# A GpSimd product for the gate weights of every second token group in a dense expert stage

## The chip, the cores and the metric

The kernel runs on one core of a Trainium2 chip. The metric is the device time of one execution in microseconds. The time before is the median of three runs; the profile is of a further execution of the same program.

## What is computed

The reference is one decoder layer on 512 tokens of width 1024: a sparse-attention head group and a gated linear recurrence side by side, one output projection, a layer norm, then a product-key expert layer (PEER) and a second layer norm. Only the expert layer matters here. Each token picks 128 of 16,384 single-neuron experts (8 heads times 16 picks), with a softmax weight for each pick:

```python
g = jax.nn.softmax(best, axis=-1)
h = jax.nn.gelu(jnp.einsum('td,thkd->thk', xb, u[experts]))
return jnp.einsum('thk,thkd->td', g * h, v[experts])
```

The inputs are float32, and all products below are float32.

## The kernel before, in words

The 512 tokens are four blocks of 128. Two ways of doing the expert layer run beside each other.

Blocks 0 and 1 are gathered (`peer_gather`, L657). For each pick k, GpSimd issues an indirect DMA (`gather`, L639) that fetches one row of 1024 numbers of table u for each of the 128 tokens, and VectorE takes its dot product with the block's activations (L663). Later the rows of table v are gathered and added up with their weights on VectorE (L676). `peer_gather` is a generator; `pump(n)` (L705) takes n rows from it at places written by hand in the rest of the program. The last 52 picks of block 0 go another way (`pe_gather`, L684): ScalarE multiplies the identity by the pick's weights into a diagonal matrix `dg` (L692), and TensorE multiplies the gathered row by it and accumulates (L694, two products of 128x512 for each row). There is one buffer for `dg`.

Blocks 2 and 3 are dense (`dense`, L714). No row is gathered: all 16,384 experts are run over these 256 tokens, and a matrix G of 128 x 128 weights for each token, zero where an expert was not picked, stands for the choice. Two stages follow one another in `dense`:

- The **G stage** (L740 to L764) builds G, four tokens at a time, in 64 groups. The picks lie on the partitions. For each group VectorE makes two one-hot tiles of 128x512 (L747), `og[0]` and `og[1]`, by comparing an iota with the two indices of every pick; both operands lie in SBUF. The picks' gate weights are multiplied into `og[1]`. In even groups ScalarE does that for three of the four tokens (L751, one 128x128 instruction for a token) and VectorE for the fourth (L753); in odd groups ScalarE does all four. TensorE then multiplies `og[0]` by `og[1]` token by token into a PSUM bank `gb` (L756), and ScalarE copies the bank of the group before into G (L734). Every third group pumps one gathered row of block 1 (GPUMP, L737; 22 in all), and 30 of the rows of `pe_gather` for block 0 are spread over the first 60 groups (L761).
- The **dense stage** (L819 to L838) streams u and v from memory in 128 rounds, splits them into two halves for precision on ScalarE and VectorE (L772, L774), and runs their products (L783, L803). It pumps the remaining gathered rows evenly.

`og[0]` has four buffers, which the u tiles of the dense stage share; `og[1]` has six. The gathered rows of both kinds share four buffers here. The two PSUM banks of the groups alternate.

The order of instructions on each engine comes from a planner that simulates the program with costs of its own and places each instruction when its operands and buffers are free; lines marked to keep program order (the dot products, the sums over gathered rows, some loads) stay in order among themselves. Each engine then runs its list strictly in order, GpSimd's gathers included, and waits by semaphores.

GpSimd does little elementwise work in the kernel before: four products of 128x512 (L267, the recurrence's gate by a norm weight that is broadcast) and four copies of 128x512 (L468), all long ahead of the G stage. L418, L419 and L676 are further VectorE work that stands near these in the trace.

Of the kernel before, what the change touches and what calls it, by code (L numbers as in the profile page):

```python
# [9 lines left out]
F32 = mybir.dt.float32  # L10
# [5 lines left out]
ALU = mybir.AluOpType  # L16
# [9 lines left out]

HGB = 5
GB = 4
UB = 4
VB = 3  # L30
HLB = 6
# [8 lines left out]
PEK2 = 38  # L40
PEPRE = 8
PEG = 60

GACTS = (3, 4)

GPUMP = 3

# [4 lines left out]
def tile_decoder_layer(ctx, tc, a, out):  # L52
    nc = tc.nc

    cst = ctx.enter_context(tc.tile_pool(name="cst", bufs=1))
    gat = ctx.enter_context(tc.tile_pool(name="gat", bufs=5))
# [66 lines left out]
    def layer_norm(ys, os_, g, b, nm):  # L123

        n = len(ys)
        mv = cst.tile([128, n, 2], F32, name="mv" + nm, tag="ln_mv", bufs=2)
        parts = [y if isinstance(y, list) else [y[:, k * 512:(k + 1) * 512] for k in range(2)] for y in ys]
        for i in range(n):
            st = cst.tile([128, 2, 6], F32, name=f"st{nm}_{i}", tag="ln_st", bufs=2)
            for k in range(2):  # L130
                nc.vector.bn_stats(st[:, k, :], parts[i][k])  # L131
            nc.vector.bn_aggr(mv[:, i, :], st)
        ve = cst.tile([128, n], F32, name="ve" + nm, tag="ln_ve", bufs=2)
        nc.vector.tensor_scalar(ve, mv[:, :, 1], EPS, None, op0=ALU.add)
        r = rsqrt(ve, n, nm)
        for i, o in enumerate(os_):
            if isinstance(ys[i], list):
                for k in range(2):
                    sl = slice(k * 512, k * 512 + 512)
                    nc.vector.scalar_tensor_tensor(o[:, sl], parts[i][k], mv[:, i, 0:1], g[:, sl],  # L140
                                                   op0=ALU.subtract, op1=ALU.mult)
            else:
                nc.vector.scalar_tensor_tensor(o, ys[i], mv[:, i, 0:1], g, op0=ALU.subtract, op1=ALU.mult)
            nc.vector.scalar_tensor_tensor(o, o, r[:, i:i + 1], b, op0=ALU.mult, op1=ALU.add)  # L144
# [487 lines left out]
    def gather(table, b, k, nm):  # L632
        n = nth[0] % (GB + len(lent))
        nth[0] += 1
        if n < GB:
            t = gat.tile([128, 1024], F32, name=f"g{nm}{b}_{k}", tag="g", bufs=GB)
        else:
            t = cst.tile([128, 1024], F32, name=f"g{nm}{b}_{k}", tag=lent[n - GB])
        nc.gpsimd.indirect_dma_start(out=t, out_offset=None, in_=table,  # L639
                                     in_offset=bass.IndirectOffsetOnAxis(ap=idx[b][k // 64][:, k % 64:k % 64 + 1], axis=0))  # L640
        return t

    def ln2_consts(nm):
        gb = []
        for i in range(2):
            t = gat.tile([128, 1024], F32, name=f"ln2_{nm}_{i}", tag="g", bufs=GB)
            nc.sync.dma_start(t, a["ln2"][None, i, :].to_broadcast([128, 1024]))
# [36 lines left out]
    def pe_gather(n, p):  # L684

        while 0 not in weighted:
            pump(1)
        ks = [pe_left.pop(0) for _ in range(n)]
        for k in ks:
            g = gather(a["v"], 0, k, "v")  # L690
            dg = gat.tile([128, 128], F32, name=f"dg{k}", tag="dg", bufs=1)
            nc.scalar.mul(dg, ident, gate[:, 0, k:k + 1])  # L692
            for i in range(2):
                nc.tensor.matmul(p[i], dg, g[:, i * 512:(i + 1) * 512], start=(k == ks[0]), stop=(k == ks[-1]))  # L694
            if k != ks[-1]:
                yield
        for i in range(2):
            y = hs[0][:, i * 512:(i + 1) * 512]
            nc.vector.tensor_tensor(y, y, p[i], op=ALU.add)
        yield  # L700
# [4 lines left out]
    def pump(n):  # L705
        while n > 0 and todo:
            try:
                if not next(todo[0]):
                    return
                n -= 1  # L710
            except StopIteration:
                todo.pop(0)

    def dense(den, dps):  # L714
# [5 lines left out]
        for i, b in enumerate(DENSE):  # L720
# [4 lines left out]
            nc.scalar.copy(t[:, 0:3, :].rearrange("p a b -> p (a b)"), p[:, :384])  # L725
            tr[b] = [t[:, n, :] for n in range(3)]
        pw = pe_gather(PEK2, [dps.tile([128, 512], F32, name=f"pw{n}", tag=f"acc0_{n}") for n in range(2)])
        for _ in range(PEPRE):
            next(pw)
# [3 lines left out]
        def evacuate(t0, p):  # L733
            nc.scalar.copy(G[:, :, t0:t0 + 4].rearrange("p j t -> p t j"), p)  # L734

        def pump_some(t0):
            if t0 // 4 % GPUMP == 0:  # L737
                pump(1)

        for t0 in range(0, T, 4):  # L740
            p = dps.tile([128, 4, 128], F32, name=f"gb{t0}", tag="gb", bufs=2)
            x = tr[DENSE[t0 // 128]]
            c = t0 % 128
            og = [den.tile([128, 4, 128], F32, name=f"og{t0}_{n}", tag=tag, bufs=bufs)
                  for n, (tag, bufs) in enumerate((("u", UB), ("hl", HLB)))]
            for n in range(2):
                nc.vector.tensor_tensor(og[n], iota[:, None, :].to_broadcast([128, 4, 128]),  # L747
                                        x[n][:, c:c + 4, None].to_broadcast([128, 4, 128]), op=ALU.is_equal)
            gact = GACTS[t0 // 4 % len(GACTS)]
            for tt in range(gact):  # L750
                nc.scalar.mul(og[1][:, tt, :], og[1][:, tt, :], x[2][:, c + tt:c + tt + 1])  # L751
            if gact < 4:
                nc.vector.tensor_tensor(og[1][:, gact:, :], og[1][:, gact:, :],  # L753
                                        x[2][:, c + gact:c + 4, None].to_broadcast([128, 4 - gact, 128]), op=ALU.mult)
            for tt in range(4):
                nc.tensor.matmul(p[:, tt, :], og[0][:, tt, :], og[1][:, tt, :], start=True, stop=True)  # L756
            if t0:
                evacuate(t0 - 4, last)
            last = p
            pump_some(t0)  # L760
            while pdone < PEK2 and pdone < PEPRE + (t0 // 4 + 1) * (PEK2 - PEPRE) // PEG:  # L761
                next(pw)
                pdone += 1
# [13 lines left out]
        def into_hidden(j, n, hp):  # L777
            u = den.tile([128, 512], F32, name=f"u{j}_{n}", tag="u", bufs=UB)
            nc.sync.dma_start(u.rearrange("p (k i) -> p k i", k=4), a["ut"][j, :, n * 4:n * 4 + 4, :])
            uh, ul = split(f"u{j}_{n}", u)  # L780
            for q, (ut, ht) in enumerate(((uh, hTl), (uh, hTh), (ul, hTh))):
                for k in range(4):
                    nc.tensor.matmul(hp, ut[:, k * 128:(k + 1) * 128], ht[n][:, k, :],  # L783
                                     start=(n + q + k == 0), stop=(n == 1 and q == 2 and k == 3))
# [18 lines left out]
                    nc.tensor.matmul(acc[i][n], wt[:, sl], vt, start=(j == 0 and q == 0), stop=(j == 127 and q == 2))  # L803

        def residual():
            ia = gat.tile([128, 128], F32, name="ia", tag="dg", bufs=1)
            nc.scalar.mul(ia, ident, ALPHA)
            for i in range(nb):
                for n in range(2):
                    for c in range(4):  # L810
                        for t in (hTl, hTh):
                            nc.tensor.matmul(acc[i][n][:, c * 128:(c + 1) * 128],
                                             t[n].bitcast(F32)[:, c, i * 128:(i + 1) * 128], ia,
                                             start=False, stop=False)
# [4 lines left out]
        for j in range(129):  # L819
# [18 lines left out]
            ws = ws_new  # L838
        ys = [gat.tile([128, 1024], F32, name=f"y{b}", tag="g", bufs=GB) for b in DENSE]
        layer_norm(acc, ys, gb[0], gb[1], "l2_dense")  # L840
# [3 lines left out]
    def stage(blocks, xT):  # L844
# [31 lines left out]
        if blocks != [0]:  # L876
            lent.clear()
            for part, tags in (("h", ("hx0", "hx1")), ("l", ("hs2", "hs3"))):
                hT_parts[part] = [cst.tile([128, 4, 256], F32R, name=f"hT{part}{i}", tag=tag) for i, tag in enumerate(tags)]
            for k in range(0, 8, 2):  # L880
                x = hT[:, k:k + 2, 128:384]
                th, tl = [hT_parts[part][k // 4][:, k % 4:k % 4 + 2, :] for part in "hl"]
                nc.scalar.copy(th, x)
                nc.vector.tensor_tensor(tl, x, th.bitcast(F32), op=ALU.subtract)
            for _ in pe_gather(PEK1, [bank(f"pv{i}", "hg") for i in range(2)]):
                pass
# [6 lines left out]
    with tc.tile_pool(name="den", bufs=1) as den, tc.tile_pool(name="dps", bufs=1, space=PSUM) as dps:  # L893
        dense(den, dps)
# [48 lines left out]
```

## Time and profile before

| what | value |
|---|---|
| median of 3 runs | 1611.0 us (1610.07 to 1612.66) |
| the profiled execution | 1606.46 us |
| its span, first to last instruction | 1604.6 us |
| busy: TensorE, VectorE, ScalarE, GpSimd | 1446.5, 1383.7, 708.0, 673.9 us |
| the G stage, first one-hot tile to the end of its last | 702.55 to 831.4 us |
| the dense stage | about 838 to 1590 us |

In the profile PE is TensorE, PEld its weight loads, DVE is VectorE, ACT is ScalarE and POOL is GpSimd. Shares over the whole span hide the stages: ScalarE is busy for 44% of the span, but in the two slices of 40 that lie wholly in the G stage it is busy for 9 tenths or more, and less in the dense stage. So a change in one stage is read from windows of that stage, and from the rows of single instructions in it. Instructions of ScalarE, VectorE and TensorE overlap by a little, so that the length of one is more than the distance from its start to the next one's. The number in square brackets behind a row is the idle time of the engine ahead of it, with what ended it.

### The profile page before, as it was taken

The numbers are of one execution on the slowest core, as the hardware profiler recorded it, in microseconds if no ns is written. First come the engines' busy times: TensorE is split into PE (matmuls) and PEld (weight loads), VectorE is DVE, ScalarE is ACT, GpSimd is POOL, SyncE is SP. The second block draws the span as 40 slices with busy tenths as digits, with TensorE's granted clock in tenths as the row PEclk, the third lists the DMA queues.
The fourth block names the chain that finished last, engine by engine and source line by source line (L and its number), as shares of the span: only waits on it lengthen the run. The fifth ranks groups of instructions, "written<-read, shape, count | busy, mean of one in ns | idle before, by whom it ended". The sixth has DMA issues, their size and how long they took to land. (4 is left out here: it accounts for less than half of the span.)

```text
span 1604.6 us, 24491 instructions
## 1 busy us (share of the span) xinstructions
PE 1446.5 (90%) x7858; PEld 1087.4 (68%) x7858; DVE 1383.7 (86%) x3263; ACT 708.0 (44%) x1501; POOL 673.9 (42%) x531
## 2 busy tenths in 40 slices
PE   8889899854788899789989999999999999999996
PEld 4568444543444565246668888888898889889995
DVE  4139999799966899998877989999998899999998
ACT  3302331122432122169984555555555555555553
POOL 0004633777744420355433444444443345534440
PEclk9999999855799899899999999999999999999998
DMA  8378987899967770467668999999999999999995
GB/s 291 125 277 301 348 268 232 290 344 330 351 242 255 263 285 11 145 203 222 218 235 301 350 340 337 353 349 352 352 357 326 336 349 362 351 352 350 355 367 189
DMA packets 166161, 467.89 MB, mean 292 GB/s; under 512 B 18576, under 2 KB 18704, under 8 KB 165904
## 3 DMA queue, kind: packets, MB, share of 16 engines
q0 software_dynamic: 73728, 268.47, 48.0%
q1 hardware_dynamic: 92304, 197.86, 34.3%
q8 instruction: 62, 1.02, 0.2%
q14 instruction: 67, 0.55, 0.1%
HBM read 464.16 MB, written 2.10 MB: 291 GB/s over the span
## 5 line engine op out<-in xcount | busy, mean ns | idle before, releaser
L639 POOL DMA_INDIRECT gv<-in_v_dram,idx x256 | 333.1, 1301 | 417.4 <-DVE hs L676 263.3
L639 POOL DMA_INDIRECT gu<-in_u_dram,idx x256 | 330.9, 1293 | 409.8 <-DVE gu L663 259.1
L663 DVE SCALAR_TENSOR_TENSOR gu<-gu,hs 128x1024 f32<-128x1024 f32 x256 | 307.2, 1222 | 28.0 <-DMA gu<-in_u_dram,idx 27.8
L676 DVE SCALAR_TENSOR_TENSOR hs<-gv,gate,hs 128x1024 f32<-128x1024 f32 x204 | 261.4, 1281 | 9.7 <-DMA gv<-in_v_dram,idx 7.8
L772 ACT CAST v_0h<-v 128x512 fp32r<-128x512 f32 x128 | 79.7, 623 | 95.7 <-PE acc L803 60.9
L523 PE MATMUL pq<-hT,wpq 128*128 128x128 f32 (+1 forms) x512 | 121.3, 396 | 0.0
L774 DVE TENSOR_TENSOR u_0l<-u,u_0h 128x512 fp32r<-128x512 f32 x128 | 88.5, 691 | 35.6 <-ACT u_0h L772 32.6
L772 ACT CAST v_1h<-v 128x512 fp32r<-128x512 f32 x128 | 79.5, 621 | 87.7 <-DMA v<-in_v_dram 42.8
L772 ACT CAST u_0h<-u 128x512 fp32r<-128x512 f32 x128 | 79.4, 620 | 78.0 <-PE hp L783 41.1
L803 PE MATMUL acc<-v_0h,wl 128*128 128x512 f32 x256 | 102.0, 399 | 4.9 <-DVE wl L793 4.9
L523 PEld LDWEIGHTS pq<-hT,wpq 128*128 128x128 f32 x512 | 81.2, 201 | 33.4 <-issue 3.9
L803 PE MATMUL acc<-v_0h,wh 128*128 128x512 f32 x256 | 101.0, 395 | 0.0
L772 ACT CAST u_1h<-u 128x512 fp32r<-128x512 f32 x128 | 79.4, 621 | 48.2 <-PE acc L803 44.6
L774 DVE TENSOR_TENSOR v_1l<-v,v_1h 128x512 fp32r<-128x512 f32 x128 | 87.8, 686 | 14.3 <-ACT v_1h L772 13.5
L803 PE MATMUL acc<-v_1h,wh 128*128 128x512 f32 x256 | 99.7, 389 | 0.0
L803 PE MATMUL acc<-v_1h,wl 128*128 128x512 f32 x256 | 99.7, 389 | 0.0
L803 PE MATMUL acc<-v_0l,wh 128*128 128x512 f32 x256 | 99.5, 390 | 0.0
L774 DVE TENSOR_TENSOR u_1l<-u,u_1h 128x512 fp32r<-128x512 f32 x128 | 87.7, 685 | 4.5 <-ACT wh L791 3.5
L783 PE MATMUL hp<-hTl,u_0h 128*128 128x256 f32 x512 | 84.3, 287 | 8.0 <-ACT u_0h L772 8.0
L783 PEld LDWEIGHTS hp<-hTl,u_0h 128*128 128x128 f32 x512 | 76.7, 189 | 20.8 <-ACT u_0h L772 12.4
L774 DVE TENSOR_TENSOR v_0l<-v,v_0h 128x512 fp32r<-128x512 f32 x128 | 88.1, 688 | 2.5 <-ACT v_0h L772 1.6
L783 PE MATMUL hp<-hTh,u_1l 128*128 128x256 f32 x512 | 83.9, 286 | 5.1 <-DVE u_1l L774 5.1
(277 smaller groups left out, 3137.9 us busy)
## 6 DMA issues: line engine op xcount, KB each, us to landing
v<-in_v_dram SPq DMA_DIRECT2D x256, 256.0 KB, 6.2
u<-in_ut_dram SPq DMA_DIRECT2D x256, 256.0 KB, 6.0
wpq<-in_w_pq_dram SPq DMA_DIRECT2D x32, 512.0 KB, 4.7
wo<-in_w_o_dram SPq DMA_DIRECT2D x16, 512.0 KB, 7.6
hfw<-in_w_hf_dram SPq DMA_DIRECT2D x8, 512.0 KB, 6.8
hqw<-in_w_hq_dram SPq DMA_DIRECT2D x8, 512.0 KB, 9.1
hiw<-in_w_hi_dram SPq DMA_DIRECT2D x8, 512.0 KB, 4.9
qaw<-in_w_qa_dram SPq DMA_DIRECT2D x8, 512.0 KB, 5.1
```

What stands on the lines that cost most here:

```text
L523: nc.tensor.matmul(qp[:, :nt], w[:, k, :], hT[:, k, :nt], start=(k == 0), stop=(k == 7))
L639: nc.gpsimd.indirect_dma_start(out=t, out_offset=None, in_=table, in_offset=bass.IndirectOffsetOnAxis(ap=idx[b][k // 64][:, k % 64:k % 64 ...
L663: nc.vector.scalar_tensor_tensor(g, g, 1.0, hs[b], op0=ALU.mult, op1=ALU.mult, accum_out=hd[:, k:k + 1]))
L676: nc.vector.scalar_tensor_tensor(hs[b], g, gate[:, b, k:k + 1], hs[b], op0=ALU.mult, op1=ALU.add))
L772: nc.scalar.copy(h, x)
L774: nc.vector.tensor_tensor(l, x, h.bitcast(F32), op=ALU.subtract)
L783: nc.tensor.matmul(hp, ut[:, k * 128:(k + 1) * 128], ht[n][:, k, :], start=(n + q + k == 0), stop=(n == 1 and q == 2 and k == 3))
L803: nc.tensor.matmul(acc[i][n], wt[:, sl], vt, start=(j == 0 and q == 0), stop=(j == 127 and q == 2))
```

## The change

In the G stage the weights are now applied in one of two ways. In odd groups one GpSimd product of 128x512 multiplies all of `og[1]` by the weights, broadcast along each token's 128 columns. In even groups ScalarE does all four tokens. VectorE's L753 is gone. The buffer of the diagonals `dg` becomes two; the dense stage's `ia`, which uses the same buffer, has two as well.

```diff
+DGB = 2
...
-GACTS = (3, 4)
...
-            dg = gat.tile([128, 128], F32, name=f"dg{k}", tag="dg", bufs=1)
+            dg = gat.tile([128, 128], F32, name=f"dg{k}", tag="dg", bufs=DGB)
...
-            gact = GACTS[t0 // 4 % len(GACTS)]
-            for tt in range(gact):
-                nc.scalar.mul(og[1][:, tt, :], og[1][:, tt, :], x[2][:, c + tt:c + tt + 1])
-            if gact < 4:
-                nc.vector.tensor_tensor(og[1][:, gact:, :], og[1][:, gact:, :],
-                                        x[2][:, c + gact:c + 4, None].to_broadcast([128, 4 - gact, 128]), op=ALU.mult)
+            if t0 // 4 % 2:
+                nc.gpsimd.tensor_tensor(og[1], og[1], x[2][:, c:c + 4, None].to_broadcast([128, 4, 128]), op=ALU.mult)
+            else:
+                for tt in range(4):
+                    nc.scalar.mul(og[1][:, tt, :], og[1][:, tt, :], x[2][:, c + tt:c + tt + 1])
...
-            ia = gat.tile([128, 128], F32, name="ia", tag="dg", bufs=1)
+            ia = gat.tile([128, 128], F32, name="ia", tag="dg", bufs=DGB)
```

## Rows read from the trace of the kernel before

**Rows 1.** Windows, G stage: busy us (instructions), granted clock, DMA share, GB/s

```profile
core 0: us, PE busy (x) PEld busy (x) DVE busy (x) ACT busy (x) POOL busy (x), PEclk, DMA share, GB/s
703.00:833.00 130.00, 121.57 (x632) 82.09 (x632) 112.74 (x207) 128.40 (x319) 60.06 (x54) 1.00 0.71 225
```

**Rows 2.** Groups, 704 to 838 us: count, busy us, mean ns, idle before, releaser

```profile
L747 DVE TENSOR_TENSOR og<-iota,dtr 128x512 f32<-128x512 f32 x126 | 79.8, 687 | 0.8 <-PE gb L756 0.7
L751 ACT ACTIVATE og<-og,dtr 128x128 f32<-128x128 f32 x224 | 74.4, 427 | 0.3 <-DVE og L747 0.2
...
L694 PE MATMUL pw<-gv,dg 128*128 128x512 f32 x128 | 63.0, 614 | 7.2 <-ACT dg L692 7.2
...
L663 DVE SCALAR_TENSOR_TENSOR gu<-gu,hs 128x1024 f32<-128x1024 f32 x22 | 26.9, 1224 | 16.2 <-DMA gu<-in_u_dram,idx 16.2
...
L692 ACT ACTIVATE dg<-ident,gate 128x128 f32<-128x128 f32 x31 | 13.3, 429 | 0.0
```

**Rows 3.** Timeline of ACT: start, length, line, count; idle before in brackets

```profile
792.49 0.39 ACT L692 ACTIVATE dg<-ident,gate 128x128 f32<-128x128 f32 x1
792.79 1.03 ACT L734 COPY G<-gb 128x512 f32<-128x512 f32 x1
793.62 0.96 ACT L751 ACTIVATE og<-og,dtr 128x128 f32<-128x128 f32 x3
794.49 1.04 ACT L734 COPY G<-gb 128x512 f32<-128x512 f32 x1
```

**Rows 4.** Timeline of PE, same stretch

```profile
796.93 1.98 PE L694 MATMUL pw<-gv,dg 128*128 128x512 f32 x4 [0.19 <-ACT dg L692]
798.75 2.06 PE L756 MATMUL gb<-og,og 128*128 128x128 f32 x16
```

**Rows 5.** Timeline of DVE: the stage's first products, one round, the stage's end

```profile
702.55 6.18 DVE L747 TENSOR_TENSOR og<-iota,dtr 128x512 f32<-128x512 f32 x10 [0.60 <-ACT dtr L725]
...
796.76 1.22 DVE L663 SCALAR_TENSOR_TENSOR gu<-gu,hs 128x1024 f32<-128x1024 f32 x1 [0.83 <-DMA gu<-in_u_dram,idx]
...
797.91 0.28 DVE L753 TENSOR_TENSOR og<-og,dtr 128x128 f32<-128x128 f32 x1
798.11 2.52 DVE L747 TENSOR_TENSOR og<-iota,dtr 128x512 f32<-128x512 f32 x4
...
803.13 1.23 DVE L663 SCALAR_TENSOR_TENSOR gu<-gu,hs 128x1024 f32<-128x1024 f32 x1 [0.96 <-DMA gu<-in_u_dram,idx]
...
831.44 0.68 DVE L699 TENSOR_TENSOR hs<-hs,pw 128x512 f32<-128x512 f32 x1
```

**Rows 6.** Windows, dense stage: busy times, clock, DMA share, GB/s, as in group 1

```profile
1400.00:1500.00 100.00, 99.57 (x641) 90.63 (x640) 95.48 (x140) 54.05 (x106) 45.43 (x33) 1.00 0.98 353
```

**Rows 7.** Timeline after the stage: ACT's first cast of the dense stage

```profile
837.13 0.62 ACT L772 CAST u_0h<-u 128x512 fp32r<-128x512 f32 x1 [3.57 <-DMA u<-in_ut_dram]
```

**Rows 8.** Timeline of POOL, HGRN2 gate products of blocks 1 and 2

```profile
274.60 2.50 POOL L267 TENSOR_TENSOR gs<-gs,ghg 128x512 f32<-128x512 f32 x2
```

**Rows 9.** Timeline of POOL, same round as DVE's in group 5

```profile
798.26 1.35 POOL L639 DMA_INDIRECT gu<-in_u_dram,idx  x1 [2.11 <-DVE og L753]
799.91 0.94 POOL L639 DMA_INDIRECT gv<-in_v_dram,idx  x1 [0.31 <-PE gb L756]
804.63 1.15 POOL L639 DMA_INDIRECT gu<-in_u_dram,idx  x1 [3.78 <-DVE gu L663]
```

**Rows 10.** Timeline of DVE over the second of these products

```profile
272.14 1.22 DVE L663 SCALAR_TENSOR_TENSOR gu<-gu,hs 128x1024 f32<-128x1024 f32 x1
...
276.19 2.00 DVE L663 SCALAR_TENSOR_TENSOR gu<-gu,hs 128x1024 f32<-128x1024 f32 x1
```

**Rows 11.** POOL copy, DVE L676 over it; L676's ns min/median/max over all

```profile
430.88 0.97 POOL L468 COPY rex<-rsm 128x512 f32<-128x512 f32 x1
...
431.42 2.83 DVE L676 SCALAR_TENSOR_TENSOR hs<-gv,gate,hs 128x1024 f32<-128x1024 f32 x2
...
L676 DVE SCALAR_TENSOR_TENSOR hs<-gv,gate,hs x204: 1270/1280/1510, 411.2 to 1576.0; 128x1024 f32<-128x1024 f32 x102
```

## The prediction

> **What bounds the kernel now.** I read the windows first, to see which engine fills the G stage. From 703 to 833 us ScalarE is busy for 128.4 of 130 us, TensorE for 121.6, VectorE for 112.7 and GpSimd for 60.1, at full clock [rows 1]. The groups then tell who waits: ScalarE's weights (L751) and diagonals (L692) have next to no idle time ahead of them, while TensorE waits 7.2 us for diagonals and VectorE 16.2 us for gathered rows [rows 2]. So ScalarE sets the pace, and TensorE stands close behind.
>
> Busy times overlap on these engines, so I take the pitch from start to start. ScalarE: three weights from 793.62 to 794.49, 0.29 us each; one evacuation from 792.79 to 793.62, 0.83; one diagonal 0.30 [rows 3]. The stage has 224 weights, 64 evacuations and 30 diagonals: 65.0 + 53.1 + 9.0 = 127.1 us, which is the stage. TensorE: one gathered row's two products take 1.82 us, and two groups' products 2.06 [rows 4]: 30 x 1.82 + 32 x 2.06 = 120.5 us. VectorE: a one-hot tile takes 0.61 us (ten in 6.18, four in 2.52), a dot product with a gathered row 1.15, an L753 multiply 0.20 [rows 5]: 128 x 0.61 + 22 x 1.15 + 32 x 0.20 = 78.1 + 25.3 + 6.4 = 109.8. VectorE's part of the stage runs from 702.55 to 831.44 [rows 5], 128.9 us, so 19 us of it are idle, 16.2 of them waits for gathers.
>
> Behind the stage, TensorE is busy for 99.6 of 100 us in the dense stage [rows 6], and its first operand is loaded into buffers that the G stage gives back, which ScalarE awaits for 3.57 us [rows 7]. Nothing there absorbs a shift; I pass a change of the G stage on to the end one to one.
>
> **What goes.** ScalarE loses 96 of its 224 weights: 27.8 us, leaving 99.3. VectorE loses the 32 multiplies of L753: 6.4 us, leaving 103.4. The second diagonal buffer costs or brings next to nothing: ScalarE did not wait for TensorE to give the first one back (idle before L692: 0.0 [rows 2]); TensorE's 7.2 us came from ScalarE's own queue, and that shortens with the 27.8 us. Were VectorE's and GpSimd's work untouched, TensorE's 120.5 us would be the next bound.
>
> **What is added.** GpSimd gets 32 products of 128x512. The same operation, shape and broadcast is in the kernel: the four at L267 take 1.27 us each, two of them in a row 2.50 [rows 8]. GpSimd has room: 54 gathers at 1.41 us (60.1 us of busy time over 54, and the 0.3 that stands even ahead of one that hardly waits, at 799.91 [rows 9]) and 32 x 1.27 are 76 + 41 = 117 us.
>
> The price lies on VectorE. While the second of these two ran (until 274.60 + 2.50 = 277.10), a dot product that started at 276.19 took 2.00 us, where the one before took 1.22 [rows 8, 10]: 0.78 of the 0.91 us that were left of the GpSimd product were lost to it. The reverse shows inside the G stage, where VectorE's one-hot tiles start at 798.11 and every 0.61 us after [rows 5]. The gather at 799.91, just ahead of the tile boundary at 799.94, took 0.94 us; the one at 798.26 took 1.35 [rows 9], and 798.26 + (1.35 - 0.94) is 798.67, where the tile from 798.11 makes way for that of 798.72. GpSimd waits for the end of a VectorE tile, and VectorE for the end of a GpSimd product. All VectorE work left in the stage is of this kind: one-hot tiles and dot products, both with two operands in SBUF. So GpSimd's products add to VectorE's time; they don't run beside it.
>
> How much of a product VectorE loses has two ends. The copy at L468 (430.88, 0.97 us) ended at 431.85, and the sum that started at 431.42 took 1.51 where 1.28 is usual [rows 11]: 0.23 lost of 0.43, about half, or 0.68 us of a 1.27 us product. The other end is the whole 1.27. The L267 row (0.78 of 0.91) is the same operation, so I take 0.86 x 1.27 = 1.10. The Trainium skill (SBUF — State Buffer, section "SBUF: two separate sides") says that the loser of the port pair is blocked for the other's whole instruction; by that the price is 1.27 and the sum 5.4 us higher. The L267 row has it a little shorter.
>
> **The sum.** VectorE: 103.4 + 32 x 1.10 = 138.6 us against the 128.9 of now: +9.7, with no idle left (ends: 103.4 + 21.8 = 125.2, -3.7; 103.4 + 40.6 = 144.0, +15.1). To this come waits for gathers, now 16.2 us. The ends are none and all of it. The dot product at 803.13 waited 0.96 us, and its gather was issued 4.87 us before at 798.26, once the dot product from 796.76 had given its buffer back [rows 5, 9]. Three groups bring 1.5 products, some 1.6 us more VectorE time between two dot products, less 0.3 for the lost L753, which by itself covers that 0.96. But a product now also stands ahead of gathers in GpSimd's in-order queue, and its 1.27 us, plus up to 0.61 until a tile ends, come on top of the 4.87 for perhaps every second gather. I take some 6 us of waiting, between the ends and nearer none. Together +16 us.
>
> The profiled execution took 1606.5 us (span 1604.6 and 1.9 around it), 4.5 below the median of the runs shown. On it the sum is 1606.5 + 16 = 1622.5; the same shift on the median gives **1627**. The forecast's own range: +6 (a price of 1.0 and no waits) to +31 (the full 1.27 and all 16.2 of the waits): 1617 to 1642.
>
> **Rivals.**
> (a) Faster. The place is the meeting of L747 and the new product; the point that decides is what one product costs VectorE. With no idle left, VectorE keeps today's 128.9 us at (128.9 - 103.4) / 32 = 0.80 us; well below that TensorE decides at 120.5, 8.4 us less than now: 1603. For it: the copy's 0.68, and VectorE's 19 idle us, in which products could fall for free. Against it: the L267 row, and the gather that waited for the tile. The Trainium skill (Advanced Engine Details and Errata, section "VectorE Performance Modes") names only GpSimd and two-port VectorE instructions as blocking each other; by that rule tiles at one element per cycle would be free, and this rival would follow. The dot product of 2.00 us in this trace speaks against it: at 1.15 us for 1024 elements it is not in a doubled mode either, and was blocked. 14%.
> (b) Nothing measurable. Dot products follow one another once in three groups, here after 6.37 us (796.76 to 803.13 [rows 5]), and this loop of gather, landing and release runs at ScalarE's pace already. If products fit into its waits at a price near 0.80, stage and time stay: 1611. 9%.
> (c) Much slower by the queue. GpSimd works in order: a gather that waits for a buffer (3.78 us at 804.63 [rows 9]) holds up the product behind it, and with it TensorE's group and the evacuation. If each of the 22 rounds loses 1 us more this way, it is 22 us on top of +9.7: 1643, with 1637 to 1665 possible. Against it: four one-hot buffers let VectorE work ahead, and the planner puts products and gathers in one order that it foresees. 17%.
> That the change doesn't do what it says has little room: the 96 weights leave ScalarE's queue whatever the planner does, and I give it no chance of its own.
>
> **The numbers.** The forecast (+6 to +31) has 60%. Slower: 60 + 17 = 77%. Faster 14%, same 9%, where 0.2% (3.2 us) is about what a measurement of this kernel can tell from no change. The range 1606 to 1648 holds the forecast, (b) and over half of (c), and leaves out (a) and the upper part of (c), a little under 2 in 10.
>
> **What would show it.** Right: dot products and one-hot tiles in the G stage that take about 1.1 us longer than the 1.22 and 0.69 of now [rows 2], some 32 of them; ScalarE with idle time and some 100 us of work; a stage that ends 10 to 20 us later, with the dense stage unchanged in length. TensorE waits for og from GpSimd. Wrong: L747 tiles at 0.69 us throughout while products run, or the products falling into VectorE's idle time; then TensorE would stand at 120 us with no gaps. Long idle times before the products, with gathers ahead of them, would show (c).

## The result and the profile after

The changed kernel took 1628.05 us (median of 7 executions, 1626.07 to 1634.13), the kernel before 1612.66 us beside it (7 executions, 1609.92 to 1621.38). The ratio is 1.0094, with a 95% interval of 1.0066 to 1.0121: slower by 15.4 us. The median of the kernel before moves from job to job (1612.7, 1621.4, 1636.7, 1618.3 and 1616.7 us in five), so below only ratios within one job are compared, and of the profiles the lengths of stages. Line numbers after are one or two smaller: L747 is now L746, L663 is L662, L692 and L694 are L691 and L693; the weights stand at L749 (GpSimd) and L752 (ScalarE).

Windows of the changed kernel, the stage and 100 us of the dense stage. The columns are those of [rows 1].

```profile
core 0: us, PE busy (x) PEld busy (x) DVE busy (x) ACT busy (x) POOL busy (x), PEclk, DMA share, GB/s
719.00:857.00 138.00, 111.54 (x605) 80.39 (x606) 137.34 (x177) 106.36 (x218) 97.71 (x80) 0.97 0.63 193
1424.00:1524.00 100.00, 98.27 (x629) 89.05 (x628) 95.05 (x138) 53.34 (x104) 47.14 (x34) 1.00 0.97 351
```

Against [rows 1] the engine without idle time is another one: VectorE, busy for 137.3 of 138 us. ScalarE has 32 us of idle time and TensorE 26. The dense stage [rows 6] is as it was.

Groups of the changed kernel from 704 to 862 us, as in [rows 2]: count, busy us, mean ns, idle time before them.

```profile
L746 DVE TENSOR_TENSOR og<-iota,dtr 128x512 f32<-128x512 f32 x128 | 109.7, 918 | 16.1 <-ACT dtr L724 15.4 <-PE gb L754 0.6
...
L693 PE MATMUL pw<-gv,dg 128*128 128x512 f32 x120 | 62.0, 641 | 32.2 <-DMA gv<-in_v_dram,idx 32.2
...
L752 ACT ACTIVATE og<-og,dtr 128x128 f32<-128x128 f32 x128 | 40.8, 390 | 16.5 <-DVE og L746 16.3
L749 POOL TENSOR_TENSOR og<-og,dtr 128x512 f32<-128x512 f32 x32 | 37.4, 1169 | 6.9 <-DVE og L746 2.6 <-PE gb L754 2.5 <-PE pw L693 1.3
...
L662 DVE SCALAR_TENSOR_TENSOR gu<-gu,hs 128x1024 f32<-128x1024 f32 x23 | 30.1, 1311 | 0.0
L691 ACT ACTIVATE dg<-ident,gate 128x128 f32<-128x128 f32 x28 | 10.9, 391 | 26.1 <-PE pw L693 25.9
```

The one-hot tiles went from 687 ns to 918, the dot products from 1224 to 1311. That is 128 x 0.231 + 23 x 0.087 = 31.6 us more VectorE time, 0.99 us for each of the 32 products. The dot products wait for nothing any more (16.2 us before). ScalarE's weights wait for VectorE. Two waits are new and, as the run e2 below shows without any product, come from the second buffer: TensorE's gathered rows wait 32.2 us for their gathers (11.4 of it ahead of the first tile), and VectorE waits 15.4 us for `dtr`, the copy of the transposed picks, ahead of its first tile.

The time of the stages follows from the starts of single instructions: the last one of VectorE's routing (the choice of each token's picks) ahead of the stage, the first and the last one-hot tile, the first and the last product of the dense stage. The two profiles at the right are one more execution of each kernel, taken together (its expectation stands with the experiments).

| us | before | after | difference | before, again | after, again | difference |
|---|---|---|---|---|---|---|
| last routing instruction | 701.7 | 703.1 | +1.4 | 705.9 | 708.6 | +2.7 |
| from there to the first one-hot tile | 0.8 | 15.7 | +14.9 | 8.8 | 16.0 | +7.2 |
| VectorE's part of the stage | 128.9 | 138.4 | +9.5 | 131.8 | 139.8 | +8.0 |
| from its end to the first dense product | 6.4 | 1.2 | -5.2 | 3.9 | 0.4 | -3.5 |
| dense products | 754.1 | 755.8 | +1.7 | 758.6 | 754.0 | -4.6 |
| span | 1604.6 | 1626.9 | +22.3 | 1621.7 | 1631.8 | +10.1 |

The two differences lie on both sides of the medians' +15.4. What they share is +8 to +9.5 in the stage, +7 to +15 ahead of it and -3.5 to -5.2 behind it.

**What a product does.** Timelines of the changed kernel: GpSimd's products first, then VectorE beside them.

```profile
781.56 1.05 POOL L749 TENSOR_TENSOR og<-og,dtr 128x512 f32<-128x512 f32 x1
787.55 1.05 POOL L749 TENSOR_TENSOR og<-og,dtr 128x512 f32<-128x512 f32 x1
...
779.45 3.72 DVE L746 TENSOR_TENSOR og<-iota,dtr 128x512 f32<-128x512 f32 x4
783.09 1.21 DVE L662 SCALAR_TENSOR_TENSOR gu<-gu,hs 128x1024 f32<-128x1024 f32 x1
...
784.23 4.93 DVE L746 TENSOR_TENSOR og<-iota,dtr 128x512 f32<-128x512 f32 x6
```

Four tiles took 2.52 us before [rows 5] and take 3.72 with one product beside them; six take 4.93 where the pitch of 0.61 makes 3.7. Either way some 1.2 us go to a product of 1.05. The dot product with no product beside it keeps its 1.21. Where the product itself took longer (1.16 us and more), the tile beside it took 1.51 instead of 1.91 and lost 0.8; the mean of 0.99 lies between the two.

One product of the 32 met other VectorE work, and it cost nothing (GpSimd, then VectorE):

```profile
844.96 1.04 POOL L749 TENSOR_TENSOR og<-og,dtr 128x512 f32<-128x512 f32 x1 [2.50 <-PE gb L754]
...
844.74 1.27 DVE L698 TENSOR_TENSOR hs<-hs,pw 128x512 f32<-128x512 f32 x2
845.94 0.68 DVE L130 BATCH_NORM_STATS2 stl<-hs 128x6 f32<-128x512 f32 x1
```

The sum L698 reads one of its operands from PSUM, and L130 has one operand. Two sums in 1.27 us is their usual pace (0.68 each, overlapping; the same sum of the kernel before took 0.68 [rows 5]). So it is VectorE's instructions with two operands in SBUF that lose time to a product here. No run was made to vary the operands; the rows of the second profile of the changed kernel and of e8 show the same.

**What stands ahead of the stage.** Timelines of the changed kernel from 692 us on: GpSimd, TensorE, ScalarE, VectorE.

```profile
692.11 11.52 POOL L638 DMA_INDIRECT gv<-in_v_dram,idx  x1 [0.30 <-PE pw L693]
...
707.52 3.75 PE L693 MATMUL pw<-gv,dg 128*128 128x512 f32 x4 [11.38 <-DMA gv<-in_v_dram,idx]
...
715.85 1.95 PE L693 MATMUL pw<-gv,dg 128*128 128x512 f32 x4 [1.85 <-DMA gv<-in_v_dram,idx]
717.64 0.38 PE L722 MATMUL dtp<-ident,ij 128*128 128x128 f32 x2
...
711.37 0.40 ACT L691 ACTIVATE dg<-ident,gate 128x128 f32<-128x128 f32 x1 [12.96 <-PE pw L693]
...
717.91 0.40 ACT L691 ACTIVATE dg<-ident,gate 128x128 f32<-128x128 f32 x1 [3.41 <-PE pw L693]
718.21 0.84 ACT L724 COPY dtr<-dtp 128x384 f32<-128x384 f32 x2
...
703.10 0.23 DVE L619 SCALAR_TENSOR_TENSOR idx<-dc_v,dc_v 128x64 uint32<-128x64 f32 x1
718.76 1.29 DVE L746 TENSOR_TENSOR og<-iota,dtr 128x512 f32<-128x512 f32 x2 [15.43 <-ACT dtr L724]
```

One gather took 11.52 us. TensorE's row (707.52) waited 11.38 us for it, and two more rows stood between that row and the last transposes of the picks (717.64). ScalarE's diagonals (L691) waited for the rows to give a buffer back, and the copy of the transposes, which every one-hot tile needs, stood behind them. In TensorE's order 11 rows stand ahead of the last transposes; in the kernel before it is 5. Nobody moved them by hand: the planner placed them earlier once there were two diagonal buffers.

In the kernel before the same stretch reads as follows (GpSimd, TensorE).

```profile
698.01 4.24 POOL L639 DMA_INDIRECT gv<-in_v_dram,idx  x1 [1.02 <-PE pw L694]
...
698.29 1.99 PE L694 MATMUL pw<-gv,dg 128*128 128x512 f32 x4 [0.55 <-ACT dg L692]
...
701.21 0.33 PE L723 MATMUL dtp<-ident,ij 128*128 128x128 f32 x1 [0.83 <-DVE ij L617]
```

The long gather (4.24 us) belongs to a row behind the transposes, so nothing that the first tile needs waits for it.

**Behind the stage** ScalarE's first cast of the dense stage, which waited 3.57 us for its u tile [rows 7], waits no more (timeline of ScalarE, changed kernel).

```profile
855.74 0.63 ACT L770 CAST u_0h<-u 128x512 fp32r<-128x512 f32 x1
```

### The profile page after: what moved, and what is told of

Same layout as the page of the kernel before. It is cut to its first block, busy times and chain, and to the rows that moved or that the text cites. A ratio compares the mean times of both kernels' runs of the same rounds, so it can differ in the third digit from the quotient of the medians.

```text
span 1626.9 us, 24442 instructions
## 1 busy us (share of the span) xinstructions
PE 1446.2 (89%) x7858; PEld 1095.7 (67%) x7858; DVE 1407.4 (87%) x3231; ACT 687.9 (42%) x1405; POOL 724.2 (45%) x563
## 3 DMA queue, kind: packets, MB, share of 16 engines
q8 instruction: 62, 1.02, 0.3%
## 5 line engine op out<-in xcount | busy, mean ns | idle before, releaser
L638 POOL DMA_INDIRECT gv<-in_v_dram,idx x256 | 348.3, 1361 | 417.5 <-DVE hs L675 264.4
L662 DVE SCALAR_TENSOR_TENSOR gu<-gu,hs 128x1024 f32<-128x1024 f32 x256 | 308.9, 1229 | 11.4 <-DMA gu<-in_u_dram,idx 11.4
L746 DVE TENSOR_TENSOR og<-iota,dtr 128x512 f32<-128x512 f32 x128 | 109.7, 918 | 16.1 <-ACT dtr L724 15.4
L693 PE MATMUL pw<-gv,dg 128*128 128x512 f32 x152 | 77.8, 642 | 41.6 <-DMA gv<-in_v_dram,idx 32.7
```

The costliest lines, as they stand in the source:

```text
L662: nc.vector.scalar_tensor_tensor(g, g, 1.0, hs[b], op0=ALU.mult, op1=ALU.mult, accum_out=hd[:, k:k + 1]))
```

## The experiments

Theory P (port): each GpSimd product stops VectorE for about its own length. Theory D (diagonals): the second buffer of diagonals itself costs time, by the order that it gives. "D1" below is the changed kernel with `DGB = 1`.

**One diagonal buffer with the products** (e1):

```diff
-DGB = 2
+DGB = 1
```

> The changed kernel with one buffer of diagonals, as before the change. Theory P (each GpSimd product takes some 1.1 us from VectorE): the G stage's VectorE part stays at about 138 us. Theory D (the second diagonal buffer is what makes the first one-hot tile start at 718.8 instead of 702.6 us): it starts near 703 again, and the time falls by 6 to 16 us from that of the changed kernel, to 1612 to 1622. Rival (the late start comes from a plan that moved because of the GpSimd products): first tile near 718 and the time of the changed kernel, 1628.

Ratio 1.0074 (1.0040 to 1.0108). Groups, 704 to 862 us:

```profile
L746 DVE TENSOR_TENSOR og<-iota,dtr 128x512 f32<-128x512 f32 x128 | 105.7, 889 | 0.6 <-ACT dtr L724 0.6
...
L662 DVE SCALAR_TENSOR_TENSOR gu<-gu,hs 128x1024 f32<-128x1024 f32 x23 | 32.1, 1394 | 11.2 <-DMA gu<-in_u_dram,idx 11.2
```

The wait ahead of the stage is gone (0.6), and the price stays: 128 x 0.202 + 23 x 0.170 = 29.8 us, 0.93 each. But 11.2 us of waits for gathers are back and the stage takes 140.1 us (with its last tile counted at the usual 0.68), with another 10.6 from its end to the first dense product. So the start near 703 came back as theory D said, but the fall of 6 to 16 us did not come: these waits took the place of the buffer's gap, and by the time alone the two kernels cannot be told apart.

**Two diagonal buffers in the kernel before** (e2):

```diff
-            dg = gat.tile([128, 128], F32, name=f"dg{k}", tag="dg", bufs=1)
+            dg = gat.tile([128, 128], F32, name=f"dg{k}", tag="dg", bufs=2)
...
-            ia = gat.tile([128, 128], F32, name="ia", tag="dg", bufs=1)
+            ia = gat.tile([128, 128], F32, name="ia", tag="dg", bufs=2)
```

> The kernel before with two buffers of diagonals and nothing else. The prediction's step (the second buffer costs or brings next to nothing): within 3 us of the kernel before, first one-hot tile near 703. Theory D: the first tile starts 10 to 16 us later and the time rises by 5 to 15 us. P says nothing of it: tiles stay at 0.69 us.

Ratio 1.0075 (1.0041 to 1.0109), without one product on GpSimd. Groups, 704 to 862 us:

```profile
L747 DVE TENSOR_TENSOR og<-iota,dtr 128x512 f32<-128x512 f32 x128 | 81.3, 685 | 33.0 <-PE gb L756 21.1 <-ACT dtr L725 11.9
...
L694 PE MATMUL pw<-gv,dg 128*128 128x512 f32 x120 | 62.6, 647 | 27.4 <-DMA gv<-in_v_dram,idx 27.3
L639 POOL DMA_INDIRECT gv<-in_v_dram,idx x28 | 31.6, 1128 | 39.5 <-PE pw L694 30.7 <-PE dtp L723 5.4 <-issue 3.0
L663 DVE SCALAR_TENSOR_TENSOR gu<-gu,hs 128x1024 f32<-128x1024 f32 x23 | 28.0, 1217 | 0.0
```

The tiles keep their 0.69 us, the first one waits 11.9 us for `dtr` (again 11 rows stand ahead of the last transposes), and within the stage rows wait for gathers while gathers wait for rows to give their buffers back. The dot products wait for nothing (0.0), with no product in the kernel. The stage takes 135.2 us. Theory D holds, for the gap and inside the stage.

**The product on VectorE**, with two buffers (e3) and with one (e5, the same edit on D1):

```diff
-                nc.gpsimd.tensor_tensor(og[1], og[1], x[2][:, c:c + 4, None].to_broadcast([128, 4, 128]), op=ALU.mult)
+                nc.vector.tensor_tensor(og[1], og[1], x[2][:, c:c + 4, None].to_broadcast([128, 4, 128]), op=ALU.mult)
```

> The changed kernel with the product of every second group on VectorE instead of GpSimd, same operands. P: a VectorE product is one more 0.61 us tile, so VectorE's part of the stage is 103.4 + 32 x 0.61 = 122.9 us instead of 138.5, and the time falls by some 10 to 16 us against the changed kernel, to about 1614, with the late start unchanged. Rival (GpSimd's products run beside VectorE and something else lengthens the stage): 32 x 0.61 = 19.5 us more on VectorE, 1640 or more.

> The changed kernel with one buffer of diagonals and the product of every second group on VectorE instead of GpSimd. P (a GpSimd product takes over 1 us from VectorE): VectorE's sum is 103.4 + 32 x 0.61 = 122.9 us where it is 138.6 with GpSimd; the stage takes 123 to 131 us (it was 140.2 in e1_dgb1), starts within 2 us of the routing's end, and the time is 9 to 17 us below e1_dgb1, at or a little below the kernel before. Rival (what held e3_vec, TensorE waiting for gathered rows, does not hang on the second buffer): a stage of over 140 us and no gain on e1_dgb1.

e3: ratio 1.0131 (1.0085 to 1.0177). e5: 0.9962 (0.9934 to 0.9990), faster than the kernel before. First two groups of e3, 704 to 862 us:

```profile
L746 DVE TENSOR_TENSOR og<-iota,dtr 128x512 f32<-128x512 f32 x122 | 76.4, 683 | 32.6 <-PE gb L754 20.5 <-ACT dtr L724 12.1
L693 PE MATMUL pw<-gv,dg 128*128 128x512 f32 x121 | 64.7, 659 | 32.1 <-DMA gv<-in_v_dram,idx 31.7
```

and the second of them in e5:

```profile
L693 PE MATMUL pw<-gv,dg 128*128 128x512 f32 x152 | 74.4, 612 | 8.8 <-ACT dg L691 4.7 <-DMA gv<-in_v_dram,idx 4.0
```

The two differ in the buffer alone: 31.7 us of waiting for gathers against 4.0, a stage of 146.4 us against 126.9, and 12.4 us ahead of it against 0.8. e3 missed its forecast of about 1614 us: its 1640.3 is the time that the rival named, though not by the rival's cause, since its products cost VectorE a tile each (0.68 us) and VectorE waited 20.5 us for TensorE to give tiles back. With two buffers e3 hides what the product's engine is worth. With one, e5 says it: VectorE does the product itself at a pitch of 0.61 us, and its stage is 13 us shorter than with GpSimd doing it (140.1 in e1). VectorE has less to do when it does the work itself.

**A product that nobody reads** (e4), added to the kernel before behind the matmuls of odd groups:

```diff
+            if t0 // 4 % 2:
+                sc = den.tile([128, 4, 128], BF, name=f"sc{t0}", tag="sc")
+                nc.gpsimd.tensor_tensor(sc, og[1], x[2][:, c:c + 4, None].to_broadcast([128, 4, 128]), op=ALU.mult)
```

> The kernel before with one extra GpSimd product of 128x512 for every second group, whose result nobody reads (it multiplies the finished one-hot tile by the weights again, into a scratch tile of its own). P: VectorE's 109.8 us become up to 109.8 + 32 x 1.1 = 145; of its 19 idle us some part is filled, so the stage grows by 5 to 16 us and one-hot tiles and dot products of some 1.8 and 2.3 us appear. Rival (no loss on VectorE): tiles stay at 0.69 us and the time within 3 us of the kernel before.

Ratio 1.0035 (1.0003 to 1.0068). Durations (min, median, max in ns) of the instructions on `og`, 710 to 862 us:

```profile
L747 DVE TENSOR_TENSOR og<-iota,dtr x128: 674/678/1922, 716.8 to 854.5; 128x512 f32<-128x512 f32 x128
L759 POOL TENSOR_TENSOR sc<-og,dtr x32: 1047/1202/1951, 722.6 to 852.1; 128x512 bf16<-128x512 f32 x32
L753 DVE TENSOR_TENSOR og<-og,dtr x32: 276/1112/1340, 724.1 to 847.9; 128x128 f32<-128x128 f32 x32
```

L753, 0.28 us before [rows 5], has a median of 1.11 us, and single one-hot tiles take 1.92; the forecast dot products of 2.3 us did not appear. Nothing reads the product, and yet VectorE's part grows to 138.3 us, as long as in the changed kernel. Against the second profile of the kernel before, which has the same 9 us between routing and stage, that is 6.5 us more. In groups the tiles have a mean of 773 ns and L753 of 759: 128 x 0.086 + 32 x 0.48 = 26 us, 0.8 for each product. It is the length of VectorE's instructions that grew, not their waits (a buffer of `og[1]` is given back later, but no tile waited for one). That is theory P with no data dependence left that could explain it.

**No product at all** (e7, on D1; the odd groups' weights are left out, half of them all):

```diff
-            if t0 // 4 % 2:
-                nc.gpsimd.tensor_tensor(og[1], og[1], x[2][:, c:c + 4, None].to_broadcast([128, 4, 128]), op=ALU.mult)
-            else:
+            if t0 // 4 % 2 == 0:
```

> The changed kernel with one buffer of diagonals and without the GpSimd product, so the odd groups' one-hot tiles stay unweighted: this leaves out half of the weights, and shows the stage with ScalarE relieved and nothing put in its place. P: VectorE 103.4 us, TensorE 120.5: a stage of 120 to 129 us, 11 to 20 below e1_dgb1, no tile over 0.75 us. Rival (the products are not what lengthens the stage): 135 us or more.

Ratio 0.9965 (0.9934 to 0.9996), a stage of 124.7 us, tiles of at most 0.72 us. VectorE now waits 21.8 us for gathers and TensorE is busy for 114 of 124 us. So in this order free products would have been worth some 4 us of stage: rival (a)'s end, a little above its 120.5. It is no floor, as e10 below does more work in a shorter stage.

**The weight fused into the comparison** (e6, on D1): VectorE's two-step instruction compares and multiplies, for each token.

```diff
+            for tt in range(4):
+                nc.vector.tensor_scalar(og[1][:, tt, :], iota, x[1][:, c + tt:c + tt + 1], x[2][:, c + tt:c + tt + 1],
+                                        op0=ALU.is_equal, op1=ALU.mult)
```

> One buffer of diagonals, no GpSimd product and no weights on ScalarE: VectorE compares and multiplies in one instruction for each token (128x128, one tensor and two column operands), for all groups. P and the sums: ScalarE falls to some 62 us; VectorE takes 64 x (0.61 + 4 x 0.20) + 25.3 = 115.5 us if such an instruction costs what L753 cost, 138 us if it costs 0.29; TensorE's 120.5 us is then the bound. Stage 120 to 131 us, time 0 to 10 us below the kernel before; at 0.29 us 10 above.

Ratio 1.0072 (1.0041 to 1.0102), a stage of 147.7 us to the end of its last fused instruction: a miss. Groups, 704 to 862 us:

```profile
L748 DVE TENSOR_SCALAR og<-iota,dtr 128x128 f32<-128x128 f32 x240 | 69.2, 355 | 0.0
```

Four of them take 1.02 us from the first's start to the next tile's (0.255 each), more than the 0.20 that was assumed. They take over ScalarE's weights too, so VectorE's sum is 64 x (0.61 + 1.02) + 22 x 1.15 = 130 us, above the 123 of e5, and 17 us of waits for TensorE to give one-hot tiles back come on top.

**No rows ahead of the stage** (e8, the changed kernel with both buffers):

```diff
-PEPRE = 8
+PEPRE = 0
```

> The changed kernel with none of block 0's gathered rows put ahead of the G stage by hand (PEPRE 0 instead of 8), two buffers. In the order of TensorE's instructions 5 such rows then stand ahead of the last transposes of the indices, where the changed kernel has 11 and the kernel before 5. Theory D (these rows, waiting for gathers, put off the first one-hot tile): the first tile follows the routing's last instruction by under 4 us instead of 15.7, and the time falls by 5 to 13 us against the changed kernel, if 8 more rows in the stage (14.6 us of TensorE's time) don't make TensorE its bound: 135 us against VectorE's 138.6. Rival (the gap hangs on something else of the second buffer): gap over 8 us, time unchanged.

Ratio 1.0077 (1.0044 to 1.0111). The gap shrinks from 15.7 to 2.1 us, and the stage grows from 138.4 to 143.4, with eight more rows in it. The gap went with the rows, as theory D said; the forecast fall of 5 to 13 us did not come, and the time cannot be told from the changed kernel's 1.0094.

**Both kernels once more**, on one chip, for the spread of the profiles:

> The kernel before, unchanged, looked at again. Theory H (a gather that GpSimd starts while VectorE runs the routing is held until VectorE lets it go; whether that happens depends on when the rows ahead of it finish, and with that on the TensorE clock they had): either the last three rows of pv run at half clock (3.8 us each) and the first one-hot tile follows the routing after 0.8 us, or they run at full clock (2.0 us), a gather is held for over 10 us, and the first tile follows after about 9 us. In both, the stage takes 127 to 131 us.

> The changed kernel, unchanged, looked at again. Theory D (the second buffer puts 11 gathered rows on TensorE ahead of the transposes): a gap of 12 to 16 us between routing and first one-hot tile again, and a stage of 137 to 140 us. Rival (the gap of 15.7 us was an accident of that one execution): a gap of under 9 us.

Their stages stand in the table above. In the second profile of the kernel before, GpSimd's and TensorE's timelines read

```profile
694.60 11.77 POOL L639 DMA_INDIRECT gv<-in_v_dram,idx  x1 [2.57 <-PE pw L694]
...
709.96 3.75 PE L694 MATMUL pw<-gv,dg 128*128 128x512 f32 x4 [8.02 <-DMA gv<-in_v_dram,idx]
713.51 0.63 PE L723 MATMUL dtp<-ident,ij 128*128 128x128 f32 x2
```

The same program with the same order lost 8.0 us ahead of the stage here: the long gather was this time one that the fifth row waits for. The prediction's 702.55 was the kernel's better case. Theory H's second case came about; the stage, 131.8 us, is a little above its range. The changed kernel kept theory D's forecast in both numbers (16.0 and 139.8).

The last row of `pv`, the accumulation of `pe_gather` ahead of this one, in the first and in the second profile of the kernel before:

```profile
683.56 3.78 PE L694 MATMUL pv<-gv,dg 128*128 128x512 f32 x4 [0.55 <-ACT dg L692]
...
688.29 1.98 PE L694 MATMUL pv<-gv,dg 128*128 128x512 f32 x4 [0.55 <-ACT dg L692]
```

The first ran at a granted clock of 0.50 to 0.53 (680 to 688 us), near the lower of the two levels, 1.2 GHz; the second at 1.00 (688 to 692 us). In both profiles TensorE had been busy for 11 to 12 of the 20 us up to 680. All nine profiles of kernels with one buffer divide the same way. Where the last three rows of `pv` all took 3.78 us (the first profile, e1, e5, e6, e10), the long gather took 4.2 us and the first tile came 0.8 us after the routing. Where the last one or two took 1.98 us (the second profile, e4, e7, e9), it took 11.8 us and the tile came 8.8 to 9.0 us after. This is read from nine profiles; no run set the clock.

**Half a product**, on D1: in odd groups two tokens by ScalarE, two by one 128x256 product, on GpSimd (e9) and on VectorE (e10):

```diff
             if t0 // 4 % 2:
-                nc.gpsimd.tensor_tensor(og[1], og[1], x[2][:, c:c + 4, None].to_broadcast([128, 4, 128]), op=ALU.mult)
-            else:
-                for tt in range(4):
-                    nc.scalar.mul(og[1][:, tt, :], og[1][:, tt, :], x[2][:, c + tt:c + tt + 1])
+                nc.gpsimd.tensor_tensor(og[1][:, 2:, :], og[1][:, 2:, :],
+                                        x[2][:, c + 2:c + 4, None].to_broadcast([128, 2, 128]), op=ALU.mult)
+            for tt in range(2 if t0 // 4 % 2 else 4):
+                nc.scalar.mul(og[1][:, tt, :], og[1][:, tt, :], x[2][:, c + tt:c + tt + 1])
```

e10 has `nc.vector` in place of `nc.gpsimd`.

> One buffer of diagonals; in odd groups GpSimd multiplies only two of the four tokens (128x256) and ScalarE the other two. P: a product half as long takes half as much from VectorE, 32 x 0.5 = 16 us less than in e1_dgb1: VectorE 103.4 + 16 = 119 us, ScalarE 99.3 + 18.6 = 118, TensorE 120.5; the stage takes 121 to 131 us (140.1 in e1_dgb1), and the time is within 5 us of the kernel before or a little under it. Rival (what a product costs is a fixed price for each hand-over between the engines): a stage of over 135 us.

> The changed kernel with one diagonal buffer, where of an odd group's four tokens ScalarE weights two and one VectorE product of 128x256 the other two: the same split as in the half product on GpSimd, with the engine changed. Theory P (a GpSimd product stops VectorE for about its own length): VectorE pays some 0.34 us for its own half product, half of the 0.61 of the full one, instead of the 0.67 that the half product on GpSimd cost it (one-hot tiles of 827 ns and dot products of 1386 where 688 and 1224 are usual). VectorE 103.4 + 32 x 0.34 = 114, ScalarE 192 x 0.29 + 53 + 9 = 118, TensorE 120.5: tiles at 0.69 throughout, a stage of 121 to 129, a ratio of 0.990 to 0.999. Rival (the load on VectorE does not matter once it is below 129 or so; waits for gathers fill what it gains): waits of 10 us or more before dot products, a stage of 128 or longer, and a ratio no lower than the 0.9962 of the full product on VectorE. If the time is as long as with the half product on GpSimd (1.006), the port was not what cost it.

e9: ratio 1.0062 (1.0033 to 1.0090), stage 140.7 us. e10: **0.9921 (0.9892 to 0.9951)**, stage 117.8 us, median 1604.6 against 1616.65. First e9's groups, 704 to 862 us:

```profile
L746 DVE TENSOR_TENSOR og<-iota,dtr 128x512 f32<-128x512 f32 x128 | 97.5, 827 | 8.8 <-ACT dtr L724 8.8
...
L662 DVE SCALAR_TENSOR_TENSOR gu<-gu,hs 128x1024 f32<-128x1024 f32 x22 | 30.5, 1386 | 15.8 <-DMA gu<-in_u_dram,idx 15.6
```

then e10's, 690 to 835 us:

```profile
L746 DVE TENSOR_TENSOR og<-iota,dtr 128x512 f32<-128x512 f32 x128 | 80.8, 683 | 0.6 <-ACT dtr L724 0.6
...
L752 ACT ACTIVATE og<-og,dtr 128x128 f32<-128x128 f32 x192 | 64.1, 422 | 0.1
...
L662 DVE SCALAR_TENSOR_TENSOR gu<-gu,hs 128x1024 f32<-128x1024 f32 x23 | 28.0, 1217 | 6.7 <-DMA gu<-in_u_dram,idx 6.7
...
L749 DVE TENSOR_TENSOR og<-og,dtr 128x256 f32<-128x256 f32 x32 | 13.3, 417 | 0.0
```

and e10's window of the stage:

```profile
706.50:823.50 117.00, 114.80 (x613) 80.27 (x613) 112.03 (x201) 116.00 (x283) 58.40 (x52) 1.00 0.75 243
```

e9 missed its forecast of 121 to 131 us, and its stage is as long as the rival said. But a fixed price for each hand-over would have left e1's 0.93 us for a product, and on GpSimd half a product costs VectorE 128 x 0.140 + 22 x 0.162 = 21.5 us, 0.67 each. That is less than a whole one costs but more than half of it, and more than VectorE's own 0.42. On VectorE no tile is lengthened; TensorE, VectorE and ScalarE are all within 5 us of the stage's 117, and the kernel is the fastest of the study. Its stage is below the forecast 121 to 129, so TensorE's sum of 120.5 us, which set the floor there and in the prediction, was too high: from its first to its last group product TensorE takes 118.0 us in e10. The engine is the only difference between the two programs' text. It accounts for 21.5 - 32 x 0.34 = 11 us of the 23 by which the stages differ (0.34 us is the half product's pitch in e10's timeline); 9 more are waits for gathers (15.6 against 6.7). Why e9 has these waits and e4 has not (1.3) no run settles. The 8.8 us ahead of e9's stage are those of the long gather.

## Why the prediction was right, and which steps were not

- **ScalarE loses 27.8 us and the bound goes to VectorE.** Right: VectorE is busy for 137.3 of 138 us, and ScalarE waits 16.3 us for L746.
- **The price, 1.10 us in the sum.** Right in mechanism and nearly in size: 0.99, in the middle between its ends of 0.68 and 1.27. The product itself is shorter (median 1.055 us) than L267's 1.27. e4 and the pairs e1, e5 and e9, e10 show that it is the engine and not a dependence. That VectorE's part came out at 138.4 us where 138.6 was forecast is luck in part: 103.4 + 31.6 is 135.0. Most of the rest is 2.5 us of block 0's closing work (L698, L130, L131), which the plan put into this stage and the kernel before had behind it. The Trainium skill (SBUF — State Buffer, section "SBUF: two separate sides") has the loser blocked for the other's whole instruction; the trace agrees: 0.99 us lost to an instruction of 1.055, and 0.67 to one of 0.625 (median of e9's half products).
- **The second rule**, from which rival (a) would have followed, falls short here. The Trainium skill (Advanced Engine Details and Errata, section "VectorE Performance Modes") names only two-port VectorE instructions as blocking and blocked by GpSimd's. In this trace one-hot tiles at 0.69 us took up to 1.92, and they run in no doubled mode, as a bf16 product of twice as many elements takes the same 0.69 us (L614 in the last section). Rival (a)'s direction fits e7, where the price is nothing and the kernel is faster by 0.35%.
- **+6 us of waits for gathers.** Wrong: 0.0 us in the changed kernel. The step that failed puts these waits down to the products alone ("a product now also stands ahead of gathers in GpSimd's in-order queue"). They follow the buffer: with two buffers they are 0.0 us with products (the changed kernel) and without (e2); with one they are 11.2 us with whole products (e1) and 15.6 with half ones (e9), so the price alone did not cover them.
- **"The second diagonal buffer costs or brings next to nothing."** Wrong, and the largest error: alone it costs 0.75% (e2). The step looked for a wait that the buffer would end, found none, and stopped there. A buffer also tells the planner that it may place rows earlier, and here it put six more of them, each with a gather, ahead of the transposes that the whole stage waits for: +7 to +15 us ahead of the stage, by how the kernel before fared in the profile that it is compared with.
- **"Nothing there absorbs a shift."** Wrong by 3.5 to 5.2 us: the later stage end found the first u tile loaded, so the 3.57 us of [rows 7] fell away.
- **The sum.** Forecast +16, measured +15.4, and that closeness is luck. With the measured price of 0.99 and no waits the prediction's own terms give +6, the lower end of its range. The rest came from terms that it had at nothing: +7 to +15 ahead of the stage by the second buffer, the closing work in it, less 4 to 5 behind it.
- **Rival (c), the queue**, did not come about: idle time ahead of the products is 6.9 us for all 32. Of the signs named, TensorE's wait for `og` from GpSimd came only once, for 2.7 us.

## What to carry to other kernels

Before moving elementwise work from VectorE or ScalarE to GpSimd, count what VectorE loses beside it: where VectorE's instructions had two operands in SBUF it was 0.8 to 1.0 us for a product of 1.05, so that VectorE was better off doing the product itself (e5, e10). Judge a second buffer by what the planner will move ahead because of it, not only by the wait that it ends, and read the order on TensorE and GpSimd at the stage's entry. Balance a stage by its three engines' sums: with one more eighth of all weights moved from ScalarE to VectorE in whole instructions of 128x256 (e10), the stage fell from 128.9 us (131.8 in the second profile) to 117.8.

## What was not expected of the hardware

A gather that GpSimd starts while VectorE runs its routing (bf16 and f32 instructions back to back, mostly with two operands in SBUF) seems to be held at times until VectorE pauses. The commonest length ahead of this stage is 0.94 us. In the changed kernel it was 11.52 (692.11 to 703.63), and VectorE's last routing instruction ended at 703.33. In the kernel before it was 4.24 (to 702.25, VectorE idle from 701.95), in its second profile 11.77 (to 706.37, VectorE idle from 706.08): each time 0.3 us after VectorE went idle. Each of the fourteen profiles has one such gather ahead of the stage, of 4.2 to 11.8 us; eleven end 0.3 us after VectorE's first pause since the gather's start, the other three (e2, e3, e8) 0.8 us after it. In e2 a gather of 7.15 us ended at 699.01, in the middle of the routing, and there VectorE had its one pause, 0.74 us up to 698.95. This timeline of e2 shows both, GpSimd first:

```profile
691.86 7.15 POOL L639 DMA_INDIRECT gu<-in_u_dram,idx  x1 [0.30 <-issue]
...
698.95 0.69 DVE L614 TENSOR_TENSOR oh<-oh,tab 128x1024 bf16<-128x1024 bf16 x1 [0.74 <-ACT tab L610]
```

Not every gather there is held (others took 0.93 to 2.32 us), and which one is depends on microseconds: in the first profile of the kernel before it was one that nothing ahead of the stage needed, in the second the fifth row's. Where the rows came a little earlier, by a higher clock or by a second buffer, the long gather held up what the first tile needed. No run took the hold itself away, so its cause on VectorE's side is read from these coincidences and not tested.
